# Sample attention of a hybrid decoder step: key pages in the prompt heads' memory, and key tiles that become the attention output's parts

## Chip, cores and metric

The kernel runs on one core of a Trainium2 chip, as one program. The metric is the device time of one execution in microseconds, given as the median of several runs. Beside each run stand the span of the profiled execution (from its first to its last recorded instruction) and the granted clock of the tensor engine.

## What is computed

One layer of a decoder trunk over 1024 prompt tokens and 64 sample tokens (8 sequences of 8). The mixer between two feed-forward networks has two branches, and each branch's output is gated:

```python
h = x + 0.5 * rms_norm(swiglu(rms_norm(x)))
q_sb, k_sb, v_sb, q_r, k_r, v_r, g_r, a_sb, a_r = split(rms_norm(h) @ w_in)
o_sb = stick_breaking(q_sb, keys, vals)        # 8 heads of 64
o_r  = silu(g_r) * head_norm(retention(rope(q_r), rope(k_r), v_r))
m = sigmoid(a_sb) * (o_sb @ w_sb_out) + sigmoid(a_r) * (o_r @ w_ret_out)
h = h + rms_norm(m @ w_o)
h = h + 0.5 * rms_norm(swiglu(rms_norm(h)))
```

For a sample, keys and values are 2048 cached positions, in 16 pages of 128 that a page table picks out of a pool, and its own new ones. Stick-breaking attention multiplies each sigmoid weight by a running product over the later positions, so logits are worked off from the newest page backwards.

## The kernel before

Precision first: nearly every large product is made of three matmuls (`mm3`, lines 133, 137, 138), on a high and a low part of each operand. The high part is made by ACT (line 96), the low part by DVE or POOL (line 99). This splitting is work that stands ahead of the matmuls all over the kernel.

The stages follow each other: the first FFN up to about 830 us; then the projections, retention and the prompt's attention (`prompt_sb`, to about 1642 us); the samples' attention (`decode_sb`, 1642 to 1940); `mixer_out` (1940 to 2097); the second FFN.

In `prompt_sb` each head holds its queries, two key parts and values in a pool `pqk` with three buffers, so three heads' tensors are there at a time. `decode_sb` opens its pools `decp` (pages: 6 buffers for keys, 5 for values, half a megabyte each), `deck` (the new keys kn, the query tile qd and two tiles kt of turned keys) and `dec` behind that. Pages come by indirect DMAs, which POOL issues (`gather`).

The samples go in four blocks of two sequences. `logits` of block g+1 runs beside `values` of block g (`both`). A key page is turned by transposes on the tensor engine (line 1202), copied from PSUM into kt by ACT or DVE in turn, and multiplied with qd (`product`, through line 1115). `stick` makes the weights bt out of a bank of logits; `weights` turns them again into at, which `values` multiplies with the value pages. A product is put off by one page group (`late`), a turn of weights by another (`todo`), and both lists are emptied at a block's end. qd is one tile: its 288 columns are cleared once by POOL (line 1106), and ACT fills in the eight query pieces of each block (line 1133).

The order on each engine is fixed when the program is built, and is for the most part that of the code. To cover waits, `through(gen, k)` puts k steps of other products, called fills, behind each step of a generator; the table `FILL_DEC` gives k for the five passes (the first logits, three mixed passes, the last values). A fill is one k-step, three matmuls, of the gates or of the product with w_ret_out (`gate_steps`, `ret_steps`), in the banks pa. For the latter the retention's output is loaded in three parts (`ul<-orT`, line 843) and split by ACT and DVE between the steps (`prep_step`).

At the end the samples' outputs odec are written into the last 64 columns of the DRAM tensor osT (line 1275), where the prompt's lie already. `mixer_out` loads osT in three column parts, sq (line 1528: 512, 288 and 288 columns), splits them into sh and sl, and multiplies them with w_sb_out into the two banks pa. DVE multiplies each result with a gate loaded from gaT (line 1545), adds the retention's from mrT (line 1546) and splits it into mh and ml, the input of the product with w_o, whose results ACT copies out as y (line 1561). y, normed, is split into the quarters q of the second FFN's input. SP issues all plain DMAs in program order, on eight lanes in turn; a DMA waits for the one eight places before it.

Of the kernel before, what the change touches and what calls it, by code (L numbers as in the profile page):

```python
# [19 lines left out]
P = 128  # L20
# [23 lines left out]
FILL_DEC = (.6, .8, .8, .8, .6)  # L44
# [24 lines left out]
class Trunk:  # L69
# [99 lines left out]
    def setup(self):  # L169
# [17 lines left out]
        self.osT = self.t(self.dram, [512, T], "osT")  # L187
# [700 lines left out]
    def prompt_sb(self):  # L888
        nc, io = self.nc, self.io
        win = io["w_in"][0]  # L890
        with ExitStack() as ctx:
            qp = self.pool("pqk", ctx)
# [12 lines left out]
            def proj(p):  # L905

                qs = [self.t(qp, [P, TP], "qs", F32R, bufs=3) for e in range(2)]
                kh = [self.t(qp, [P, TP], "kh", F32R, bufs=3) for e in range(2)]
                kl = [self.t(qp, [P, TP], "kl", F32R, bufs=3) for e in range(2)]
                vs = [self.t(qp, [P, 8, P], "vs", F32R, bufs=3) for e in range(2)]  # L910
# [159 lines left out]
    def decode_sb(self):  # L1070
# [5 lines left out]
        with ExitStack() as ctx:  # L1076
            pp = self.pool("decp", ctx)
            kp_ = self.pool("deck", ctx)
            dp = self.pool("dec", ctx)
# [11 lines left out]
            kn = self.t(kp_, [P, 4, TD], "kn")  # L1091
# [32 lines left out]

            def logits(g, ats):


                qv = qd.rearrange("q (b x) -> q b x", x=144)[:, :, :P].rearrange("q b (m y) -> q b m y", y=32)
# [31 lines left out]
                def new_keys():  # L1160
# [4 lines left out]
                    bt = self.t(dp, [P, TD], "btn")  # L1165
# [5 lines left out]
                    nc.scalar.activation(atn[:TD], tp[:TD, :P], AF.Copy)  # L1171
# [11 lines left out]
                def product(ps, b2, j, kt):  # L1183
                    side_by_side(ps, partial(query, b2), lambda m: kt[:, m, :], b2 == 0, b2 == 1)
                    if b2:
                        bt = self.t(dp, [P, 512], "bt", bufs=2)
                        left[0] = stick(bt, ps.rearrange("q (h i x) -> q h x i", h=2, i=2), 512, left[0])
                        todo.append((j, bt))

                late, todo, left = [], [], [None]  # L1190
                nk = new_keys()
                step = 0
                for j in range(NG - 1, -1, -1):
                    ps = self.bank("pb")
                    for b2 in range(2):
                        kp = [gather(self.t(pp, [P, 1024], "page", bufs=6), ck, 2 * g + b2, 2 * j + x)
                              for x in range(2)]
                        kt = self.t(kp_, [P, 4, 512], "kt", bufs=2)
                        for m in range(4):
# [18 lines left out]
                        late.append((ps, b2, j, kt))  # L1218
# [615 lines left out]
```

## Time and profile before

| | us |
|---|---|
| median of 3 runs | 2893.32 |
| lowest and highest run | 2891.1 and 2895.43 |
| the profiled execution | 2891.72 |
| its span | 2889.2 |
| PE busy in the span | 2798.6 (97%) |
| DVE, ACT, POOL busy | 2017.1, 1245.3, 738.5 |

The mean granted clock of the profiled execution is 0.99. In the profile PE is the tensor engine's matmuls, PEld its weight loads, DVE the vector engine, ACT the scalar engine, POOL GpSimd and SP the engine that issues most DMAs. An idle time is put down to what ended it, after the sign "<-". The time around the span is 2.5 us.

### The profile page before, as it was taken

To read this page: it belongs to the slowest core of one execution; us is meant where nothing else is said; L and a number is where in the kernel's file an instruction comes from. 1 tells how busy PE (TensorE), PEld (TensorE's weight loads), DVE (VectorE), ACT (ScalarE), POOL (GpSimd) and SP (SyncE) were. 2 spreads that over 40 slices of the span, in tenths; PEclk is the share of its full clock that TensorE was granted. 3 is DMA by queue.
4 is the path that set the end of the run, shared out by engine and by line. 5 is a ranking of instruction groups with operands and counts; after the bars stand their busy time and mean duration, and the time that the engine had idled before them with its cause. 6 is when DMAs were issued, how large, how long until landed. Compare 5 with 4: busy or idle time off the path is not lost.

```text
span 2889.2 us, 51617 instructions
## 1 busy us (share of the span) xinstructions
PE 2798.6 (97%) x20064; PEld 2633.3 (91%) x20064; DVE 2017.1 (70%) x3922; ACT 1245.3 (43%) x2546; POOL 738.5 (26%) x679
## 2 busy tenths in 40 slices
PE   7999999999999999999999889989999999999998
PEld 7898899999999999989999867768989988999997
DVE  7888878888753553546888744436578888688776
ACT  6444444444343333335666543213354444544443
POOL 0234513333150000000000245520013334233321
PEclk9999999999999999999999999999999999999999
DMA  6444444333252322333222389876333336333431
GB/s 177 145 127 144 140 155 123 110 112 108 80 162 83 99 84 86 94 113 80 76 74 76 123 294 332 297 244 198 105 96 121 119 110 189 122 103 107 130 89 42
DMA packets 420420, 380.63 MB, mean 132 GB/s; under 512 B 30352, under 2 KB 380944, under 8 KB 420176
## 3 DMA queue, kind: packets, MB, share of 16 engines
q1 hardware_dynamic: 397904, 306.03, 34.6%
q0 software_dynamic: 22272, 71.31, 7.4%
q8 instruction: 157, 2.57, 0.4%
q14 instruction: 87, 0.71, 0.1%
HBM read 310.03 MB, written 63.05 MB: 129 GB/s over the span
## 4 chain that ended last, share of the span: by engine, by line
PE 59%; DVE 5%; DMA 3%; issue 2%; POOL 1%; ACT 1%; SPq 0%; DVEq 0%; POOLq 0%; ACTq 0%
PE pa L133 10%; PE pa L138 10%; PE pa L137 10%; PE pb L133 3%; PE pb L138 3%; PE pb L137 3%; PE pc L137 3%; PE pc L138 3%; PE pc L133 3%; PE pc L1202 2%; PE pm L1011 1%; PE pm L1115 1%; PE pc L999 1%; DVE sl L99 1%; DMA ul<-orT 1%
## 5 line engine op out<-in xcount | busy, mean ns | idle before, releaser
L96 ACT ACTIVATE sh<-wr 128x512 fp32r<-128x512 f32 x592 | 340.0, 624 | 364.1 <-POOL wr L590 135.5
L133 PE MATMUL pa<-uh,wh 128*128 128x384 f32 (+1 forms) x1408 | 476.7, 339 | 4.2 <-ACT qdec L920 2.0
L138 PE MATMUL pa<-uh,wl 128*128 128x384 f32 (+1 forms) x1408 | 464.4, 330 | 0.0
L137 PE MATMUL pa<-ul,wh 128*128 128x384 f32 (+1 forms) x1408 | 463.5, 329 | 0.4 <-POOL ul L99 0.4
L99 DVE TENSOR_TENSOR sl<-wr,sh 128x512 fp32r<-128x512 f32 x592 | 398.8, 701 | 60.2 <-ACT sh L96 56.8
L133 PE MATMUL pa<-q,sh 128*128 128x256 f32 (+1 forms) x1408 | 410.4, 292 | 15.7 <-DVE p L648 7.8
L137 PE MATMUL pa<-q,sh 128*128 128x256 f32 (+1 forms) x1408 | 409.5, 291 | 2.2 <-DVE q L99 2.2
L138 PE MATMUL pa<-q,sl 128*128 128x256 f32 (+1 forms) x1408 | 408.5, 290 | 0.3 <-DVE sl L99 0.3
L137 PE MATMUL pc<-hl,whd 128*128 128x256 f32 (+2 forms) x1088 | 350.4, 324 | 2.6 <-DVE hl L99 2.6
L138 PE MATMUL pc<-hh,wld 128*128 128x256 f32 (+2 forms) x1088 | 350.0, 323 | 0.0
L133 PE MATMUL pc<-hh,whd 128*128 128x256 f32 (+2 forms) x1088 | 343.6, 324 | 4.5 <-DVE y L718 2.5
L718 DVE TENSOR_TENSOR y<-y,pc 128x256 f32<-128x256 f32 (+2 forms) x496 | 250.1, 516 | 135.8 <-PE pc L138 133.9
L133 PE MATMUL pb<-q,sh 128*128 128x288 f32 (+1 forms) x1088 | 314.8, 290 | 6.5 <-ACT sh L96 4.9
L138 PE MATMUL pb<-q,sl 128*128 128x288 f32 (+1 forms) x1088 | 314.6, 289 | 0.5 <-DVE sl L99 0.4
L137 PE MATMUL pb<-q,sh 128*128 128x288 f32 (+1 forms) x1088 | 314.9, 290 | 0.0
L133 PEld LDWEIGHTS pa<-q,sh 128*128 128x128 f32 x1408 | 268.2, 191 | 20.8 <-DVE p L648 8.8
L133 PEld LDWEIGHTS pa<-uh,wh 128*128 128x128 f32 x1408 | 265.7, 189 | 20.1 <-issue 10.0
L137 PEld LDWEIGHTS pa<-q,sh 128*128 128x128 f32 x1408 | 268.0, 190 | 4.7 <-DVE q L99 2.7
L137 PEld LDWEIGHTS pa<-ul,wh 128*128 128x128 f32 x1408 | 265.7, 189 | 3.3 <-issue 1.4
L138 PEld LDWEIGHTS pa<-q,sl 128*128 128x128 f32 x1408 | 267.2, 190 | 1.5 <-DVE sl L99 0.5
L138 PEld LDWEIGHTS pa<-uh,wl 128*128 128x128 f32 x1408 | 265.2, 188 | 2.7 <-issue 1.7
L588 POOL TENSOR_TENSOR wr<-wr 128x512 f32<-128x512 f32 x76 | 108.2, 1424 | 495.5 <-DVE sl L99 495.4
(340 smaller groups left out, 5958.3 us busy)
## 6 DMA issues: line engine op xcount, KB each, us to landing
wr<-in_w_ffn_gu_dram SPq DMA_DIRECT2D x176, 512.0 KB
wrd<-in_w_ffn_down_dram SPq DMA_DIRECT2D x88, 512.0 KB
wr<-in_w_in_dram SPq DMA_DIRECT2D x56, 512.0 KB
q<-cB SPq DMA_DIRECT2D x16, 576.0 KB
wr<-in_w_o_dram SPq DMA_DIRECT2D x10, 512.0 KB
cB<-y SPq DMA_DIRECT2D x32, 144.0 KB
cB<-xr SPq DMA_DIRECT2D x32, 144.0 KB
s<-in_state_ret_dram SPq DMA_DIRECT2D x16, 256.0 KB
```

The costliest lines, as they stand in the source:

```text
L96: return self.nc.scalar.activation(dst, src, AF.Copy)
L99: (eng or self.nc.vector).tensor_tensor(dst, src, hi.bitcast(F32), op=ALU.subtract)
L133: ins = mm(ps, wh, xh, start=first, stop=False)
L137: mm(ps, wh, xl, start=False, stop=False)
L138: mm(ps, wl, xh, start=False, stop=last)
L588: tt(v1, v0, v1, op=ALU.add)
L718: nc.vector.tensor_tensor(y[p][:, d, c], y[p][:, d, c], ps[:, :n], op=ALU.add)
L999: nc.tensor.transpose(tp[:, j * P : (j + 1) * P], bt[:, j * P : (j + 1) * P], self.ident)
L1011: ins = nc.tensor.matmul(po[:, lo:256], vs[:, j, :], ats[j // 4][x][:, j % 4, lo:256], start=(j == 0 and x == 0), stop=(j == last and x == 1))
L1115: return nc.tensor.matmul(out[32 * m : 32 * m + 32], w(m), x(m), start=first, stop=last, skip_group_check=True)
L1202: ins = nc.tensor.transpose(tp[:, i * P : (i + 1) * P], kp[i // 2][:, (i % 2) * 512 + m * P : (i % 2) * 512 + (m + 1) * P], self.ident)
```

## The change

Memory: the prompt's pool becomes three pools, pqk0 to pqk2, one for each head that is held. In the samples' stage their room holds three pools: dec2 has key pages 0 to 3; dec1 value pages 0 to 3; dec0 has kn, the two tiles qd, btn, one atn, key pages 4 and 5 and value page 4. A page can be fetched as soon as the heads that lay there have been read for the last time. The two tiles kt lie at the other end of memory, in a pool that stays open into `mixer_out`, where they become sh and sl of the first 512 columns.

Work: `late` and `todo` are no longer emptied at the end of a block; the next block's steps take them up, and a new generator `last_block`, which runs beside the last values, takes the last ones and then loads and splits the prompt's 512 columns of osT. The samples' outputs go to a DRAM tensor of their own, osD. atn and vnew have 64 rows in place of 128, which removes three memsets. In `mixer_out` the pools m1 and mg change places, and the parts 1 and 2 are loaded whole (two DMAs for each, and two for the samples' columns) and split ahead of the first product. `FILL_DEC` has other values.

```diff
-FILL_DEC = (.6, .8, .8, .8, .6)
+FILL_DEC = (.8, .8, .8, .75, .5)
...
-        self.osT = self.t(self.dram, [512, T], "osT")
+        self.osT = self.t(self.dram, [512, TP], "osT")
+        self.osD = self.t(self.dram, [512, TD], "osD")
...
-            qp = self.pool("pqk", ctx)
+            places = [self.pool(f"pqk{i}", ctx) for i in range(3)]
...
+                at = [places[(2 * p + e) % 3] for e in range(2)]
...
-            pp = self.pool("decp", ctx)
-            kp_ = self.pool("deck", ctx)
-            dp = self.pool("dec", ctx)
+            p0, p1, p2, dp = (self.pool(x, ctx) for x in ("dec0", "dec1", "dec2", "dec"))
+            key_pages = [(p2, f"kp{i}") for i in range(4)] + [(p0, f"kp{i}") for i in range(4, 6)]
+            value_pages = [(p1, f"vp{i}") for i in range(4)] + [(p0, "vp4")]
+            with self.tc.using_default_side("right"):
+                self.kpc = ExitStack()
+                kp_ = self.pool("deck", self.kpc)
+            key_parts = [(kp_, f"kt{i}") for i in range(2)]
...
-            qd = self.t(kp_, [P, 288], "qd")
-            nc.gpsimd.memset(qd, 0.0)
-            atns = [self.t(dp, [P, P], f"atn{x}") for x in range(2)]
+            qds = [self.t(p0, [P, 288], f"qd{x}") for x in range(2)]
             for x in range(2):
-                nc.gpsimd.memset(atns[x][64:128], 0.0)
+                nc.gpsimd.memset(qds[x], 0.0)
+            atns = [self.t((p0, dp)[x], [TD, P], f"atn{x}") for x in range(2)]
...
                             if late and m == 1:
-                                product(*late.pop(0))
+                                late.pop(0)()
                             if todo and b2 == 1:
-                                weights(*todo.pop(0))
+                                todo.pop(0)()
...
-                while late:
-                    product(*late.pop(0))
+            def last_block():
+                late.pop(0)()
+                for _ in range(4):
+                    yield
+                todo.pop(0)()
                 yield
-                while todo:
-                    weights(*todo.pop(0))
+                sh, sl = (in_turn(key_parts, [P, 4, 512], F32R) for _ in range(2))
+                self.first = sh, sl
+                self.attn_parts(sh, sl, 0, 512)
                 yield
...
-                    self.through(values(g, ats), FILL_DEC[4])
+                    self.through(both(last_block(), values(g, ats)), FILL_DEC[4])
...
-            nc.sync.dma_start(self.osT.rearrange("(m q) t -> q m t", q=P)[:, :, TP:T], ost)
+            nc.sync.dma_start(self.osD.rearrange("(m q) t -> q m t", q=P), ost)
...
+    def attn_parts(self, sh, sl, o, n):
+        lf = sl.bitcast(F32)
+        m = min(n, TP - o)
+        for q in range(0, 4, 2):
+            qq = slice(q * P, (q + 2) * P)
+            self.nc.sync.dma_start(lf[:, q : q + 2, :m], self.osT[qq, o : o + m].rearrange("(k p) t -> p k t", p=P))
+            if m < n:
+                self.nc.sync.dma_start(lf[:, q : q + 2, m:], self.osD[qq, :].rearrange("(k p) t -> p k t", p=P))
+        for q in range(4):
+            self.hi(sh[:, q, :], lf[:, q, :])
+            self.lo(sl[:, q, :], lf[:, q, :], sh[:, q, :])
...
             m0 = self.pool("m0", ctx)
+            m1 = self.pool("m1", ctx)
             gp = self.pool("mg", ctx)
-            m1 = self.pool("m1", ctx)
```

What this does to the order on three engines. POOL at the start of the samples, before (page and vpage are gathered pages, wl a weight's low part for a fill):

```order
L99 TENSOR_TENSOR wl_3508_19147<-wr_3506_19144,wh_3507_19146 128x1024
L1109 MEMSET atn0_3517_19205 64x128
...
L1100 DMA page_3520_19214<-in_cache_k_dram,rowix_4_75 128x1024
...
L1100 DMA page_3541_19314<-in_cache_k_dram,rowix_4_75 128x1024
L1100 DMA vpage_3619_19719<-in_cache_v_dram,rowix_4_75 128x1024
...
L1100 DMA vpage_3646_19901<-in_cache_v_dram,rowix_4_75 128x1024
L99 TENSOR_TENSOR wl_3669_20020<-wr_3667_20017,wh_3668_20019 128x1024
L1106 MEMSET qd_3516_19203 128x288
```

POOL there with the change (kp and vp are the pages):

```order
L1113 DMA kp0_3522_19228<-in_cache_k_dram,rowix_4_75 128x1024
...
L1113 DMA kp3_3533_19285<-in_cache_k_dram,rowix_4_75 128x1024
L99 TENSOR_TENSOR wl_3509_19155<-wr_3507_19152,wh_3508_19154 128x1024
L1120 MEMSET qd0_3517_19217 128x288
...
L1113 DMA kp4_3543_19333<-in_cache_k_dram,rowix_4_75 128x1024
L1113 DMA kp5_3544_19335<-in_cache_k_dram,rowix_4_75 128x1024
L1113 DMA vp4_3649_19931<-in_cache_v_dram,rowix_4_75 128x1024
L1113 DMA vp0_3623_19751<-in_cache_v_dram,rowix_4_75 128x1024
...
L1113 DMA vp3_3646_19900<-in_cache_v_dram,rowix_4_75 128x1024
L99 TENSOR_TENSOR wl_3662_19990<-wr_3660_19987,wh_3661_19989 128x1024
```

The first gathers stand ahead of the first weight split, and the memsets of qd between the gathers in place of behind them all.

SP at the end of the samples, before (wr is raw w_o, mrT and gaT are the gates' rows):

```order
L146 DMA wr_4119_22958<-in_w_o_dram 128x8x128
L1275 DMA osT_8_79<-odec_3513_19195 128x4x64
L1528 DMA sq_4013_22306<-osT_8_79 128x512
L874 DMA mrT_13_84<-gs_4000_22268 128x320
...
L1528 DMA sq_4016_22318<-osT_8_79 128x512
L1542 DMA xr_4038_22391<-gaT_10_81 128x512
L1544 DMA xr_4039_22393<-mrT_13_84 128x512
```

SP there with the change:

```order
L1296 DMA osD_9_80<-odec_3514_19209 128x4x64
L146 DMA wr_4110_22959<-in_w_o_dram 128x8x128
L1536 DMA sl1_4013_22329<-osT_8_79 128x2x288
...
L1536 DMA sl2_4015_22341<-osT_8_79 128x2x224
L1538 DMA sl2_4015_22341<-osD_9_80 128x2x64
...
L1538 DMA sl2_4015_22341<-osD_9_80 128x2x64
L146 DMA wr_4114_22991<-in_w_o_dram 128x8x128
L1572 DMA xr_4029_22391<-gaT_11_82 128x512
```

The loads of gates, xr, now stand behind the loads of both later parts and behind one more load of w_o.

ACT at the start of the second FFN, before (q are the FFN's input quarters, sh weight parts, pb the last products with w_o):

```order
L1561 ACTIVATE y1_4110_22890<-pb_4184_23488 128x288
...
L96 ACTIVATE q00_4195_23719<-y0_4109_22886 128x256
...
L1561 ACTIVATE y1_4110_22890<-pb_4189_23546 128x288
L96 ACTIVATE q01_4197_23721<-y0_4109_22886 128x256
...
L1561 ACTIVATE y1_4110_22890<-pb_4190_23572 128x288
L96 ACTIVATE sh_4211_23766<-wr_4209_23762 128x512
...
L1561 ACTIVATE y1_4110_22890<-pb_4191_23598 128x288
```

ACT there with the change:

```order
L1592 ACTIVATE y1_4101_22891<-pb_4181_23573 128x288
L96 ACTIVATE sh_4202_23767<-wr_4200_23763 128x512
...
L1592 ACTIVATE y1_4101_22891<-pb_4184_23651 128x288
L1592 ACTIVATE y1_4101_22891<-pb_4185_23677 128x288
L96 ACTIVATE q00_4186_23720<-y0_4100_22887 128x256 x4
...
L96 ACTIVATE q02_4190_23724<-y0_4100_22887 128x256 x4
L96 ACTIVATE sh_4215_23856<-wr_4213_23852 128x512
```

The sixteen splits of y stand behind the last copy out of pb, in place of between the tenth and the twelfth of its sixteen.

## Rows read from the trace of the kernel before

**Rows 1.** The page: the span, and busy time by engine (share of the span, instructions).
```profile
span 2889.2 us, 51617 instructions
...
PE 2798.6 (97%) x20064; PEld 2633.3 (91%) x20064; DVE 2017.1 (70%) x3922; ACT 1245.3 (43%) x2546; POOL 738.5 (26%) x679
```

**Rows 2.** Waits of PE, 1600 to 2120 us: total us, times, longest.
```profile
PE pc L999 <- DVE pt L1047: 3.3, 2, 2.0
PE pc L1115 <- POOL qd L1106: 3.1, 1, 3.1
PE pc L1179 <- DVE bt L1157: 3.0, 1, 3.0
...
PE pc L1202 <- DVE at L1180: 2.0, 1, 2.0
PE pc L1202 <- ACT btn L1152: 1.4, 1, 1.4
```

**Rows 3.** Three windows: length, busy us by engine, PEclk, DMA share, GB/s.
```profile
1640.00:1660.00 20.00, 16.65 (x103) 15.67 (x104) 2.49 (x6) 4.71 (x12) 13.42 (x15) 0.84 0.81 298
1716.00:1915.00 199.00, 198.79 (x1984) 149.38 (x1986) 89.20 (x152) 58.30 (x107) 105.19 (x96) 1.00 0.87 300
1940.00:1960.00 20.00, 12.04 (x45) 9.19 (x44) 11.40 (x20) 7.15 (x14) 0.00 (x0) 0.83 0.87 289
```

**Rows 4.** Timeline of POOL: start, us, engine, operation [idle before <- releaser].
```profile
1640.28 0.34 POOL L1109 MEMSET atn<- 64x128 f32 x2 [23.47 <-DVE bt L1050]
...
1654.95 2.34 POOL L99 TENSOR_TENSOR wl<-wr,wh 128x1024 fp32r<-128x1024 f32 x1
1657.24 0.34 POOL L1106 MEMSET qd<- 128x288 f32 x1
```

**Rows 5.** Timeline of PE around the wait on qd: page transposes.
```profile
1653.69 1.03 PE L1202 MATMUL pc<-ident,page 128*128 128x128 f32 x8
...
1658.67 1.97 PE L1202 MATMUL pc<-ident,page 128*128 128x128 f32 x8
```

**Rows 6.** Chain of waits through the first block: start, us, what.
```profile
1669.09 6.69 DMA ul<-orT
...
1703.15 11.22 DMA ul<-orT
```

**Rows 7.** Timeline of ACT: the copies into qd.
```profile
1657.61 0.70 ACT L1133 ACTIVATE qd<-qdec 64x32 f32<-64x32 f32 x4 [2.47 <-POOL qd L1106]
```

**Rows 8.** Timeline of PE at the start of mixer_out.
```profile
1947.88 1.22 PE L133 MATMUL pa<-sh,wh 128*128 128x512 f32 x2 [7.64 <-ACT sh L96]
1948.90 0.63 PE L137 MATMUL pa<-sl,wh 128*128 128x512 f32 x1
...
1955.66 0.51 PE L133 MATMUL pa<-sh,wh 128*128 128x512 f32 x1 [0.32 <-DVE xr L1545]
1956.00 0.40 PE L137 MATMUL pa<-sl,wh 128*128 128x512 f32 x1
```

**Rows 9.** Chain of waits at the end of the samples: start, us, what.
```profile
1935.07 4.11 DMA wr<-in_w_o_dram
...
1942.99 4.12 DMA sq<-osT
```

**Rows 10.** Timeline of DVE and SP there (SPq issues DMAs).
```profile
1940.38 1.22 DVE L99 TENSOR_TENSOR wlo<-wr,who 128x1024 fp32r<-128x1024 f32 x1 [3.17 <-ACT who L96]
...
1942.12 0.52 SPq L1275 DMA_DIRECT2D osT<-odec  x1
...
1945.41 0.43 SPq L1542 DMA_DIRECT2D xr<-gaT  x1
```

**Rows 11.** Timeline of ACT and DVE at the second FFN's start.
```profile
2077.51 2.65 ACT L96 ACTIVATE q<-y 128x256 fp32r<-128x256 f32 x8
...
2081.94 5.45 DVE L99 TENSOR_TENSOR q<-y,q 128x256 fp32r<-128x256 f32 x16
...
2096.80 0.41 ACT L1561 ACTIVATE y<-pb 128x288 f32<-128x288 f32 x1 [2.79 <-PE pb L138]
```

More of the change, by code (lines that the diff above doesn't have):

```diff
@@ L905, in proj @@
             def proj(p):
[L907 to L910, printed above, removed]
+                at = [places[(2 * p + e) % 3] for e in range(2)]
+                qs = [self.t(x, [P, TP], "qs", F32R) for x in at]
+                kh = [self.t(x, [P, TP], "kh", F32R) for x in at]
+                kl = [self.t(x, [P, TP], "kl", F32R) for x in at]
+                vs = [self.t(x, [P, 8, P], "vs", F32R) for x in at]
                 for e in range(2):
@@ L1076, in decode_sb, with in_turn @@
         with ExitStack() as ctx:
-            pp = self.pool("decp", ctx)
-            kp_ = self.pool("deck", ctx)
-            dp = self.pool("dec", ctx)
+            p0, p1, p2, dp = (self.pool(x, ctx) for x in ("dec0", "dec1", "dec2", "dec"))
[5 more added lines that the diff above has]
+            key_parts = [(kp_, f"kt{i}") for i in range(2)]
+            def in_turn(places, shape, dtype=F32):
+                places.append(places.pop(0))
+                return self.t(places[-1][0], shape, places[-1][1], dtype)
             mask = self.t(dp, [P, 4, TD], "dmask")
@@ L1089, in decode_sb @@
             ost = self.t(dp, [P, 4, TD], "odec")
-            kn = self.t(kp_, [P, 4, TD], "kn")
+            kn = self.t(p0, [P, 4, TD], "kn")
             tp = self.bank("pc")
@@ L1123, in side_by_side @@
                 return ins
+            late, todo = [], []
             def logits(g, ats):
+                qd = qds[g % 2]
                 qv = qd.rearrange("q (b x) -> q b x", x=144)[:, :, :P].rearrange("q b (m y) -> q b m y", y=32)
@@ L1170, in new_keys @@
                     nc.tensor.transpose(tp[:TD, :P], bt, self.ident)
-                    nc.scalar.activation(atn[:TD], tp[:TD, :P], AF.Copy)
+                    nc.scalar.activation(atn, tp[:TD, :P], AF.Copy)
                     ats[NG] = atn
@@ L1187, in product @@
                         left[0] = stick(bt, ps.rearrange("q (h i x) -> q h x i", h=2, i=2), 512, left[0])
-                        todo.append((j, bt))
-                late, todo, left = [], [], [None]
+                        todo.append(partial(weights, j, bt))
+                left = [None]
                 nk = new_keys()
@@ L1195, in logits @@
                     for b2 in range(2):
-                        kp = [gather(self.t(pp, [P, 1024], "page", bufs=6), ck, 2 * g + b2, 2 * j + x)
+                        kp = [gather(in_turn(key_pages, [P, 1024]), ck, 2 * g + b2, 2 * j + x)
                               for x in range(2)]
-                        kt = self.t(kp_, [P, 4, 512], "kt", bufs=2)
+                        kt = in_turn(key_parts, [P, 4, 512])
                         for m in range(4):
@@ L1217, in logits @@
                             yield
-                        late.append((ps, b2, j, kt))
-                while late:
-                    product(*late.pop(0))
+                        late.append(partial(product, ps, b2, j, kt))
+            def last_block():
[3 more added lines that the diff above has]
+                todo.pop(0)()
                 yield
-                while todo:
-                    weights(*todo.pop(0))
+                sh, sl = (in_turn(key_parts, [P, 4, 512], F32R) for _ in range(2))
+                self.first = sh, sl
+                self.attn_parts(sh, sl, 0, 512)
                 yield
@@ L1500, in mixer_in @@
                 self.knew = self.t(kp, [64, 512], "knew")
-                self.vnew = self.t(kp, [P, 512], "vnew")
+                self.vnew = self.t(kp, [64, 512], "vnew")
                 self.qdec = self.t(kp, [P, 4, TD], "qdec")
-                nc.gpsimd.memset(self.vnew[64:128, :], 0.0)
                 self.prompt_sb()
@@ L1514, in mixer_out @@
             m0 = self.pool("m0", ctx)
+            m1 = self.pool("m1", ctx)
             gp = self.pool("mg", ctx)
[L1516 removed]
+            self.t(gp, [P, 512], "sq", bufs=4)
             wp = self.pool("mw", ctx, bufs=2)
@@ L1522, in mixer_out @@
                 sh, sl = {}, {}
-                for c, (o, n) in reversed(list(enumerate(mch))):
+                sh[0], sl[0] = self.first
+                for c, (o, n) in list(enumerate(mch))[1:]:
                     sh[c], sl[c] = (self.t(op, [P, 4, n], f"s{x}{c}", F32R) for x in "hl")
-                for c, (o, n) in enumerate(mch):
-                    for q in range(4):
-                        raw = self.t(gp, [P, 512], "sq", bufs=4)
-                        nc.sync.dma_start(raw[:, :n], self.osT[q * P : (q + 1) * P, o : o + n])
-                        self.hi(sh[c][:, q, :n], raw[:, :n])
-                        self.lo(sl[c][:, q, :n], raw[:, :n], sh[c][:, q, :n])
+                    self.attn_parts(sh[c], sl[c], o, n)
                 w1 = [self.unit(io["w_sb_out"][0][:, j * 256 : (j + 1) * 256].rearrange("(k p) c -> p k c", p=P))
@@ L1548, in mixer_out @@
                         self.lo(ml[c][:, d, :n], m[:, :n], mh[c][:, d, :n])
+            self.kpc.close()
             y, pl, yc = self.right()
```

4 lines of the change are left out of this document (2 added, 2 removed).

## The prediction

> **What bounds the kernel now.** I read the page first: the tensor engine is busy for 97% of a span of 2889.2 us [rows 1], so a change that leaves the matmuls as they are can only win back idle time of that engine, or time in which its clock was low. The list of its waits from 1600 to 2120 us then says how much lies in the stages that the diff touches [rows 2]: besides the row of 3.3 us on the prompt's last splits there are 3.1, 3.0, 2.0 and 1.4 us around the first sample block, and one long wait at the end of the samples' stage, 7.64 us ahead of the first product with w_sb_out [rows 8]. Third, the table of windows [rows 3]: between 1716 and 1915 us the engine is busy for 198.79 of 199 us, so in the middle of the stage there is nothing to win, though the DMA engines are there at a share of 0.87; around the first and the last wait the granted clock is 0.84 and 0.83, that is, part of those windows ran at the lower of the two levels. The waits are priced with what follows them: after the wait on qd, eight page transposes take 1.97 us where the same eight took 1.03 us before it [rows 5]; after the 7.64 us, a 512-wide matmul takes 0.63 us where it later takes 0.40 [rows 8], for eight matmuls, about 1.8 us.
>
> The forecast is a sum against the profiled execution, 2891.7 us (2889.2 of span and 2.5 around it). The median of the runs shown, 2893.3, lies 1.6 us above it.
>
> **Start of the samples: +3.3 us.** Before, POOL runs two memsets of atn at 1640.28, held for 23.47 us by the prompt's last split, then eleven gathers, then a weight split of 2.34 us at 1654.95, and only then the memset of qd at 1657.24 [rows 4]; the tensor engine waits 3.1 us for it. Now the memsets of qd stand ahead of seven of the gathers, behind a wait that the prompt releases early. The 3.1 us go, and with them 0.9 us of low clock (1.97 less 1.03). Against it: the eight small ACT copies into qd, 0.70 us for four [rows 7], now run beside the prompt's last splits, for which the tensor engine is already waiting; I charge 0.7. Bounds 2.6 (all 1.4 us charged) to 4.0.
>
> **First block: +2.0 us.** The 2.0 us wait at 1678 is behind ACT and DVE, which split the first retention part when its load lands, 6.69 us after issue at 1669.09 [rows 6]. Now most gathers are issued before the prompt ends, so they no longer share the DMA engines with the loads behind them, and the fills that free this load's buffer are spent sooner (.8 of a fill a step in place of .6); I estimate an issue near 1660, 9 us earlier. The stall loses its cause, but the same splits could hold an earlier product: between -2.0 and +3.5 (2.0 and as much low clock as in the first case, rounded up).
>
> **First block edge: +2.0 us.** The logits' tail is no longer drained at the block's end; the last product and the last weights become the first work of the next block, with fills between them. That aims at the 3.0 us (transposes right behind the scan that makes bt) and touches the 1.4 us. The second retention part still arrives there, 11.22 us after issue in the trace [rows 6], and holds ACT in its queue. Of 4.4 us I take a little under half; bounds 0 and 4.4.
>
> **Last block: -0.3 us.** The splits of the prompt's part (four of ACT, four of DVE, same sizes as before) now stand inside the last block, two of DVE's ahead of the copy that makes the last weights. The transposes and the copy have fills around them, and two of the four DVE splits come only behind the copy; nothing to 3.0 us, which is what such transposes waited at the first block's edge [rows 2], taken near the small end.
>
> **End of the samples: +2.5 us.** This is the largest term. Call the end of the last fill t0: 1947.88 less 7.64, or 1940.24. Before, the third row of outputs (d = 2) starts at 1955.66, t0 + 15.4 [rows 8]. Now the first two rows need only the prompt's part and start at t0. The third needs one of two PSUM banks back, and for that DVE must multiply by a gate (line 1575 in the new text). Two chains stand ahead of that multiply. *On DVE*: eight splits of parts 1 and 2, the last four of which wait for osD to be written and read back. The odec copies no longer stand behind the w_o split that ran at 1940.38 [rows 10], so the write is issued at about t0 - 1.3; taking 4.1 us for each landing (the w_o and sq rows of the chain [rows 9]), 0.7 us of issuing and 2.2 us of splits, the multiply is free at t0 - 1.3 + 4.1 + 0.7 + 4.1 + 2.2 = t0 + 9.8. *On SP*: the loads of gates stand behind the fourth w_o load, which waits for the third to land; the third is issued when the split of 1940.38 is over, t0 + 1.4, so the gate is issued at t0 + 5.9 and lands at t0 + 10.0 (before, the first gate's load was issued at 1945.41, t0 + 5.2, and hidden [rows 10]). With 0.7 us for the multiply the third row starts at t0 + 10.7; the first two rows take 24 matmuls, 5.6 us at the full clock (7.78 from 1947.88 to 1955.66, less 0.3 of waiting and 1.8 of low clock). That is a new wait of some 5.1 us, and it brings the 1.8 us of low clock with it again, which the 15.4 already contained: 15.4 - 10.7 - 1.8 = 2.9, taken as 2.5, since the loads share the engines. Bounds: with landings of 6.69 us, the slower row, the DVE chain gives t0 + 15.7 and a loss of 2.1; with landings of half the rows' 4.1 a gain of about 7.
>
> For pieces this small the rows show only a floor: the write of odec has the same 256-byte pieces and nothing waited for it. The Trainium skill (DMA: Bandwidth & Descriptors, Specifications) says that transfers under 512 B are done as read-modify-write and do not reach line rate, which speaks against the new 256-byte reads from osD: by it this term would lie towards its lower bound. The same page (Anatomy of one DMA) puts the fixed part of a transfer at about 2.0 us; by that alone the multiply would start near t0 + 7.6, the term would be 5.3, and the sum 11.0. The 4.1 us of the rows, under load, decide.
>
> **Start of the second FFN: -1.3 us.** Pools m1 and mg change places, so the quarters of the FFN's input now lie over m1, which is read up to the last product with w_o. Before, ACT's splits of y ran from 2077.51, long before the last eviction at 2096.80 [rows 11], and matmuls of the FFN stood between those of w_o. Now all sixteen follow the last eviction: 0.41 for it, 0.33 for the first high part (2.65 by 8), 0.34 for the first low part (5.45 by 16), or 1.1 us, and 0.2 for the next weights' splits behind them. Bounds 0.5 and 3.0.
>
> **Sum.** 3.3 + 2.0 + 2.0 - 0.3 + 2.5 - 1.3 = 8.2 us: 2883.5 on the profiled scale, **2885.1** as a median. The terms' bounds give about 2875 at the good end, of which I take 2877; all bad ends together, -7.5, would be 2901; two thirds of the way there, some 2896, is as far as I think several of them go at once.
>
> **Rivals.** *(1) The waits only move.* ACT's retention splits hold other products, the edge keeps its 4.4 us, and the third row of outputs waits as long as the first did: only the start and the FFN count, 3.3 - 1.3 = 2.0, which gives 2891.3, no change. For it: the load latencies are the same DMAs in the same queues. Against: two of the waits have causes that are simply gone. Chance 0.28.
> *(2) The stalls vanish.* Gates arrive early and the parts are split in time: 3.1 + 3.0 + 2.0 + 1.4 + 7.6 + 0.9 + 1.8 = 19.8 us, 2873.5. Against: the two chains above. Chance 0.08.
> *(3) Pages come late in the last two blocks.* The fill rates go from .8 to .75 over 69 steps and from .6 over 35 steps to .5 over 41, while the first block takes more: some 5 us of cover leave the last two blocks, where the DMA engines already have a share of 0.87 [rows 3]. If that share reaches 1.0 there, the tensor engine waits for pages, 5 us and about 0.9 us of low clock after each of four waits, 3.6; and the same load makes each landing 6.69 us, so the end term falls by 4.6 to -2.1. Then 8.2 - 13.2 = -5.0, or with the last block's 3.0 us in place of 0.3, -7.7: 2901, slower. It decides where these blocks show waits on pages and less than full busy time; before, at 0.87, they show 0.21 us of idle time in 199. Chance 0.12.
> My forecast has 0.52.
>
> **How the numbers follow.** A change under about 0.2% (5.8 us) cannot be told from none in a measurement of this kernel: faster is below 2887.5, slower above 2899.1. The forecast's own spread puts about a seventh of it above 2887.5 (0.07): faster 0.45 + 0.08 = 0.53, same 0.07 + 0.28 = 0.35, slower 0.12. The range from 2877 to 2896.5 leaves out the second and third rivals.
>
> **What would show it.** No wait on qd near the first sample block and the DMA share spread over the prompt's last 20 us; the first w_sb_out product without a wait, then one of 4 to 7 us ahead of the third row on DVE (sl or xr); a wait of about 1 us on ACT or DVE's q at the first matmul of the second FFN. I am wrong if the third row does not wait, if the middle blocks show waits on pages, or if the FFN's start costs more than 3 us.

## The result, and the profile after

The change is a little slower: 2899.48 us (median of 9 runs, 2893.3 to 2903.56) against 2893.32 (9 runs), a ratio of 1.0022 with a 95% interval from 1.0012 to 1.0032. The forecast was 2885.1, with a range from 2877 to 2896.5, so the result lies above it.

The page of the change, first the span, then busy time by engine:

```profile
span 2895.6 us, 51608 instructions
...
PE 2810.4 (97%) x20064; PEld 2631.2 (91%) x20064; DVE 2016.8 (70%) x3922; ACT 1242.2 (43%) x2546; POOL 737.2 (25%) x677
```

The span is 6.4 us longer [rows 1], but the tensor engine is not idle for longer: its busy time grew by 11.8 us at the same 20064 matmuls, so it idles for 5.4 us less. The loss lies in busy time. To find its place, both executions are cut at the same four instructions: the transposes of the new keys (the start of the samples' stage), the end of the last fill (t0), the first matmul of the third row of outputs, and the fourth hidden tile of the second FFN (its multiply on DVE).

| | before, us | change, us | difference |
|---|---|---|---|
| start to the samples' stage | 1641.24 | 1641.62 | +0.4 |
| samples' stage, to t0 | 299.00 | 303.94 | +4.9 |
| t0 to the third row of outputs | 15.42 | 13.36 | -2.1 |
| third row to the fourth hidden tile | 164.19 | 167.50 | +3.3 |

The windows of the samples' stage (length, busy us of PE, PEld, DVE, ACT, POOL, then PEclk, DMA share, GB/s), before:

```profile
1641.24:1940.24 299.00, 286.72 (x2761) 219.71 (x2760) 124.32 (x216) 90.18 (x170) 146.32 (x136) 0.98 0.85 294
```

and with the change:

```profile
1641.62:1945.56 303.94, 296.39 (x2761) 216.15 (x2761) 126.84 (x222) 90.34 (x166) 133.88 (x125) 1.00 0.81 276
```

The same number of matmuls, 2761, keeps the engine busy for 9.67 us more, although the granted clock is higher (1.00 against 0.98) and the idle time fell from 12.28 to 7.55 us. So the waits did go, as the list of PE's waits between 1600 and 2150 us says; beside it stand [rows 2]:

```profile
PE pa L133 <- DVE xr L1575: 7.6, 1, 7.6
PE pc L1217 <- ACT kt L1224: 3.8, 3, 1.8
PE pc L1001 <- DVE pt L1049: 3.2, 2, 2.0
PE pb L1127 <- DVE kt L1222: 2.6, 1, 2.6
...
PE pa L133 <- ACT q L96: 0.8, 1, 0.8
...
PE pc L1217 <- ACT btn L1167: 0.3, 1, 0.3
PE pc L1217 <- DVE at L1195: 0.3, 1, 0.3
```

No wait on qd is left, none on bt at the first block's edge, and the wait on at is 0.3 in place of 2.0. In their place are 3.8 and 2.6 us on the copies of turned keys into kt. The first row is the new one ahead of the third row of outputs.

Where the busy time went is read from the timeline of PE. A stretch of the change (start, us):

```profile
1773.83 0.31 PE L137 MATMUL pa<-ul,wh 128*128 128x320 f32 x1
1773.97 0.31 PE L138 MATMUL pa<-uh,wl 128*128 128x320 f32 x1
1774.21 0.43 PE L1127 MATMUL pm<-vp,at 128*32 128x128 f32 x8
1774.57 0.41 PE L133 MATMUL pa<-uh,wh 128*128 128x320 f32 x1
1774.82 0.30 PE L137 MATMUL pa<-ul,wh 128*128 128x320 f32 x1
1774.96 0.31 PE L138 MATMUL pa<-uh,wl 128*128 128x320 f32 x1
```

A k-step's three matmuls of 128x320 follow each other at 0.15 us. Here the third one, at 1773.97, is followed after 0.24 us by eight narrow matmuls of a value product (128*32: 32 output columns of the array, four side by side), the next fill starts 0.36 us after them, and its first matmul takes 0.25. The kernel before has fewer such single lots. Counted over the samples' stage in the order of PE, it has 105 separate runs of narrow matmuls, 65 of them a single lot of eight; the change has 129, and 93 of them single. A long run of the kernel before:

```profile
1772.23 1.74 PE L1115 MATMUL pm<-vpage,at 128*32 128x128 f32 x56
1773.90 0.74 PE L1179 MATMUL pc<-ident,bt 128*128 128x128 f32 x4
```

56 narrow matmuls in 1.67 us are 0.030 each, 0.24 for eight. A separate lot of eight among fills thus costs 0.09 us ahead of it, 0.12 behind it, and 0.10 on the next full matmul: 0.31 us for each change to narrow matmuls and back. Every single lot of eight value matmuls between two fills takes 0.36 us from its start to the next fill's, 26 times before and 46 times with the change.

The same reckoning over the whole stage takes, for each run, the spacings from the last full matmul ahead of it to the second one behind it, without idle time, and subtracts the median spacings that the same matmuls have among their like in all thirteen traces. It gives 31.2 us for the 105 runs before and 38.3 us for the 129 of the change, 0.30 us a run in both, so 7.1 of the 9.67 us lie there. Some 3.7 us more lie in one place of the change, where the order has pulled a product with kt apart and set matmuls of the new keys' value product (vnew) between its pairs:

```profile
1727.10 1.04 PE L1127 MATMUL pb<-kt,qd 128*32 128x512 f32 x2
1728.07 0.41 PE L1127 MATMUL pm<-vnew,atn 64*32 64x128 f32 x4
1728.41 1.04 PE L1127 MATMUL pb<-kt,qd 128*32 128x512 f32 x2
...
1731.03 1.05 PE L1127 MATMUL pb<-kt,qd 128*32 128x512 f32 x2
1732.00 0.74 PE L1194 MATMUL pc<-ident,bt 128*128 128x128 f32 x4
```

Each pair takes 0.97 us by itself, where all eight take 0.86 when they stand together. The whole place takes 4.9 us, the same matmuls in two lots about 1.2. The kernel before has no such place; experiments 3 and 4 below have the same one, 1 and 6 a smaller one, the others none. All other spacings of the stage together came to some 1.2 us less.

The Trainium skill (TensorEngine Tiling (Array Packing), Key Properties) has a rule that fits these rows: "Changing tiling mode (not just tile) drains the TensorE". It gives no price. By that rule the order of narrow and full matmuls counts, and the three gaps above are its price here as far as these spacings show it. Whether the drain itself makes the gaps, or the loading of the next weights, no run separates. The rule was there to be weighed before the prediction, and was not.

### The profile page after: what moved, and what is told of

It reads as the page before. It is cut to its first block, busy times and chain, and to the rows that moved or that the text cites. A ratio compares the mean times of both kernels' runs of the same rounds, so it can differ in the third digit from the quotient of the medians.

```text
span 2895.6 us, 51608 instructions
## 1 busy us (share of the span) xinstructions
PE 2810.4 (97%) x20064; PEld 2631.2 (91%) x20064; DVE 2016.8 (70%) x3922; ACT 1242.2 (43%) x2546; POOL 737.2 (25%) x677
## 4 chain that ended last, share of the span: by engine, by line
PE 59%; DVE 5%; DMA 2%; issue 2%; POOL 1%; ACT 0%; SPq 0%; POOLq 0%; DVEq 0%; ACTq 0%
PE pa L133 10%; PE pa L138 10%; PE pa L137 10%; PE pb L133 3%; PE pb L138 3%; PE pb L137 3%; PE pc L137 3%; PE pc L138 3%; PE pc L133 3%; PE pc L1217 2%; PE pm L1013 1%; PE pc L1001 1%; PE pm L1127 1%; PE pb L1127 1%; DVE sl L99 1%
```

## The experiments

Two theories stood against each other. *Switching*: every separate run of narrow matmuls among full ones costs about 0.3 us, and the change cut the same work into more runs. *Place*: narrow matmuls became slower in themselves, because of where the pages now lie or what the DMA engines do beside them. Since the time up to the samples' stage varied from 1641 to 1648 us between executions of kernels that are all but the same up to there, the experiments are compared by stage, from one profiled execution of each. All ratios are to the kernel before on the same chip, with their 95% intervals. Experiments 1 to 4, 5 to 8 and 9 to 11 ran on three chips, where the kernel before has medians of 2894.71, 2901.37 and 2893.89 us; stages and ratios from different chips are compared with that reserve.

| kernel | runs | stage | PE busy | ratio |
|---|---|---|---|---|
| before | 105 | 299.00 | 286.72 | |
| change | 129 | 303.94 | 296.39 | 1.0022 (1.0012 to 1.0032) |
| 1 lists emptied | 96 | 298.49 | 286.42 | 1.0001 (0.9990 to 1.0013) |
| 2 before, lists carried | 120 | 306.14 | 294.43 | 1.0013 (1.0001 to 1.0024) |
| 3 gates first | 129 | 305.32 | 297.57 | 1.0016 (1.0004 to 1.0029) |
| 4 pools back | 129 | 302.70 | 297.04 | 0.9997 (0.9985 to 1.0008) |
| 5 before, fours | 78 | 321.02 | 289.31 | 1.0070 (1.0056 to 1.0084) |
| 6 emptied, pools back | 96 | 301.83 | 284.93 | 0.9970 (0.9959 to 0.9982) |
| 7 pairs, pools back | 92 | 295.21 | 284.37 | 0.9939 (0.9922 to 0.9956) |
| 8 fours, emptied, pools back | 75 | 320.41 | 288.10 | 1.0019 (1.0007 to 1.0031) |
| 9 before, carried, pairs | 92 | 287.19 | 280.72 | 0.9961 (0.9949 to 0.9973) |
| 10 before, pairs | 92 | 306.20 | 287.00 | 1.0027 (1.0017 to 1.0038) |
| 11 as 7, other rates | 87 | 298.11 | 284.48 | 0.9970 (0.9959 to 0.9982) |

**1. Lists emptied at the block's end again.**

```diff
                         late.append(partial(product, ps, b2, j, kt))
+                while late:
+                    late.pop(0)()
+                yield
+                while todo:
+                    todo.pop(0)()
+                yield
...
             def last_block():
-                late.pop(0)()
                 for _ in range(4):
                     yield
-                todo.pop(0)()
                 yield
```

> The change, but late and todo are emptied at each block's end again; memory, fill table and everything else stay. Theory (switching): a run of narrow matmuls (128*32) between full ones costs some 0.3 us, and the instruction order of the samples' stage has 96 such runs here, 129 in the change, 105 in the kernel before. So PE's busy time from the prompt's last transposes to the first w_sb_out product falls by about 33 x 0.31 = 10 us against the change's 295.8, some idle time comes back at the block's first edge (about 3), and the total falls by 5 to 9 us, to 2891 to 2895. Rival (place): narrow matmuls are slower because of where pages lie or of the gathers beside them; then busy time stays within 2 us of the change's and the total rises by the idle time that comes back, to 2900 to 2903.

Busy time fell by 10.0 us for 33 runs, idle time came back (12.1 us), and the total is that of the kernel before. The pages stayed where the change puts them, so *place* does not explain the busy time. The narrow matmuls themselves say the same: eight value matmuls inside a run take 0.242 us (median) before and with the change.

**2. The kernel before with the carried lists alone.**

```diff
                             if late and m == 1:
-                                product(*late.pop(0))
+                                late.pop(0)()
...
-            qd = self.t(kp_, [P, 288], "qd")
+            qds = [self.t(kp_, [P, 288], f"qd{x}") for x in range(2)]
...
-                while late:
-                    product(*late.pop(0))
-                yield
-                while todo:
-                    weights(*todo.pop(0))
-                yield
...
-                    self.through(values(g, ats), FILL_DEC[4])
+                    self.through(both(last_block(), values(g, ats)), FILL_DEC[4])
```

> The kernel before with only the carried lists: the last products and weights of a block are taken up by the next block's steps (two tiles qd, which that needs); memory, pages, fill table, osT and mixer_out as before. Order: 120 runs of narrow matmuls in place of 105. Theory (switching): PE busy in the samples' stage rises by about 15 x 0.31 = 4.7 us, the idle time there falls by 0 to 4 us, the total is 2893 to 2898. Rival (place): busy time unchanged within 1.5 us and the total falls by the idle time, to 2889 to 2893.

With the old memory, 15 runs more took 7.7 us more of busy time, and the total rose by 0.13%, barely clear of noise. The product with kt is not pulled apart here; the fill table is that of the kernel before. The two experiments undo and do the same part, from either kernel; the stage window of each, first experiment 1, then 2:

```profile
1641.31:1939.80 298.49, 286.42 (x2760) 221.27 (x2760) 124.88 (x220) 89.17 (x165) 135.81 (x125) 0.97 0.82 280
```

```profile
1646.10:1952.24 306.14, 294.43 (x2761) 219.97 (x2760) 121.76 (x218) 88.93 (x169) 144.27 (x137) 0.97 0.84 287
```

**3. Gates loaded first.** The loads and splits of parts 1 and 2 are pinned behind the second row of outputs (`beside` holds them behind what stands before them on each engine):

```diff
-                    self.attn_parts(sh[c], sl[c], o, n)
...
                         self.lo(ml[c][:, d, :n], m[:, :n], mh[c][:, d, :n])
+                        if c == 0 and d == 1:
+                            for x in (1, 2):
+                                self.beside(partial(self.attn_parts, sh[x], sl[x], *mch[x]),
+                                            PINNED + (mybir.EngineType.SP,))
```

> The change, but the loads and splits of parts 1 and 2 of the attention's output stand behind the first two rows of outputs of mixer_out on SP, ACT and DVE, so that the first gates are loaded ahead of them. If the 7.6 us wait of the third row is the gate's load behind these six loads (issued 6.6 us after the first product and 5.9 in flight), that wait falls to 2 to 4 us and the total by 3.5 to 5.5 us, to 2894 to 2896. If it is the fourth w_o load that holds the gate, the wait stays above 5.5 us and the total falls by less than 2.

A miss by halves: the wait fell from 7.59 to 4.95 us, the stretch from t0 to the fourth hidden tile from 180.86 to 178.45, and the total by too little to be told. Most of what held the gate was still there: it was issued 3.7 us behind t0, after two loads of w_o, and landed 6.16 us after issue, with none of the six loads ahead of it:

```profile
1951.67 0.37 SPq L146
1952.04 0.05 issue
1952.09 6.16 DMA xr<-gaT
```

**4. Pools m1 and mg in their old order.**

```diff
             m0 = self.pool("m0", ctx)
-            m1 = self.pool("m1", ctx)
             gp = self.pool("mg", ctx)
+            m1 = self.pool("m1", ctx)
```

> The change with the pools m1 and mg in their old order, so that the second FFN's input quarters lie over mg and m0 again and can be split before the last products with w_o. If the swap costs what the prediction says, the 0.8 us wait at the second FFN's first matmul goes and the time from the third row of outputs to that FFN's first hidden tiles falls by 1.3 to 2 us; the total by as much (2897.5 to 2898.2, hardly to be told in the total, so the profile decides). If the swap costs nothing, both stay as they are.

The wait on q went, but the stretch behind t0 fell by 3.9 us, twice what was expected, because the 7.6 us wait went too. SP's timeline shows how:

```profile
1949.46 0.43 SPq L1296 DMA_DIRECT2D osD<-odec  x1
1950.24 0.39 SPq L1572 DMA_DIRECT2D xr<-gaT  x1
1950.94 0.37 SPq L1536 DMA_DIRECT2D sl<-osT  x1
```

The first gate is issued 0.5 us ahead of t0 (1950.70), not 6.6 behind it. In the change the buffers of the gates, in mg, lie over the room of dec0 (kn, the tiles qd, key pages 4 and 5, value page 4); in the old order they do not. The trace of the change shows no wait for these tenants: the last value matmuls end at 1935.7, and the gate's load is issued at 1952.20. So the swap changes where SP has the gate's load in its order; that the shared places are the reason is not shown. Two smaller waits took its place, from the list of PE's waits:

```profile
PE pb L133 <- ACT mh L96: 2.7, 1, 2.7
PE pa L133 <- DVE gs L874: 2.3, 1, 2.3
```

**5. The kernel before with value products in fours.**

```diff
                             self.marks.append(ins.ins)
-                            yield
+                            if j == NG or i == 3:
+                                yield
```

> The kernel before with one edit of the order: four value products (two pages) are issued behind each other before the generator gives way to a fill, with fill rates raised to match (.6, 1.3, 1.3, 1.3, 1.9). No memory place, tensor or stage of mixer_out changes. Order: 78 runs of narrow matmuls in place of 105. Theory (switching, 0.31 us a run): PE busy in the samples' stage falls by about 8 us from 287.0, idle time may grow by 0 to 5 us since pages are needed in bigger lots; total 4 to 8 us below the kernel before. Rival (place and traffic decide the narrow matmuls' cost): busy time within 2 us of before, total the same or slower by the idle time.

Slower, against the expectation: the runs fell to 78, but idle time rose to 31.7 us, the granted clock over the stage fell to 0.95 (0.98 before), and busy time rose by 2.6 us. The largest waits are those at the block ends:

```profile
PE pc L1179 <- DVE bt L1157: 20.5, 4, 6.3
```

That no fills are left there for the last scan of a block, with fewer steps, is my reading and was not tested alone. This says nothing against switching, but neither for it.

**6. Lists emptied, pools back** (edits 1 and 4 together).

> The change with both parts that cost something undone: lists emptied at each block's end (96 runs of narrow matmuls) and m1 and mg in their old order. If the two costs are separate, the stretch from the prompt's last transposes to the second FFN's fourth hidden tile is that of the first experiment less what the fourth gained behind the samples' stage: 298.5 + 176.9 = 475.4 us against 478.6 before and 484.8 in the change; total 2 to 4 us below the kernel before. If they overlap, 478 to 480 and no difference in the total.

The costs did not overlap: the stretch took 472.10 us where 475.4 were expected, and the total fell by 0.30%, some 9 us, where 2 to 4 were expected. The sum hides two misses. The stage had 4.8 us more idle time than in the first experiment, and the stretch behind t0 took 170.27 us, far less than the 176.9 of the fourth; no wait is left ahead of the third row, and why is not shown.

**7. Value products in pairs, pools back, lists carried as in the change.**

```diff
-FILL_DEC = (.8, .8, .8, .75, .5)
+FILL_DEC = (.8, 1.08, 1.08, 1.02, .9)
...
                             self.marks.append(ins.ins)
-                            yield
+                            if j == NG or i % 2:
+                                yield
```

> The change with the lists carried over as it has them, m1 and mg in their old order, and value products issued in pairs (fill rates .8, 1.08, 1.08, 1.02, .9): 92 runs of narrow matmuls, so the carried lists without their cost. Theory (switching): the samples' stage takes 303.9 - 37 x 0.31 = 292.4 us with the change's idle time of about 7 us, the stretch to the fourth hidden tile 469, total 8 to 11 us below the kernel before. Rival: carrying itself (waits of ACT and DVE moved into other products) is what slows it, not the runs; then the stage stays above 299 us and the total is within 3 us of before.

Against the fourth experiment the pairs and their fill rates are the only difference in the kernel: 37 runs fewer and no product pulled apart, 12.7 us less of busy time (0.34 us a run), 5.2 us more idle, and 7.5 us off the stage. The stage took 2.8 us more than forecast, the stretch, 465.17 us, 3.8 less. Its ratio, 0.9939, is the lowest, and it beats both kernels; the total fell by some 17.5 us where 8 to 11 were forecast, though the stretch is only 13.4 us below that of the kernel before. Experiment 9, on another chip, has the lower median (2881.40 against 2883.82 us) and an interval that overlaps, so neither is shown to be the faster. The stage window of experiment 7:

```profile
1648.33:1943.54 295.21, 284.37 (x2760) 219.82 (x2760) 126.06 (x220) 89.41 (x166) 132.50 (x125) 1.00 0.83 285
```

**8. Lists emptied, fours, pools back.** Edits 1, 4 and 5, with the rates (.8, 1.28, 1.28, 1.28, 1.5).

> As the sixth experiment, with value products in fours (fill rates .8, 1.28, 1.28, 1.28, 1.5): 75 runs of narrow matmuls, lists emptied. Theory (switching): the stage takes 298.5 - 21 x 0.31 = 292 us, of it 12 us idle if the pages keep up; total 8 to 10 us below the kernel before. If pages in fours come too late, idle time rises by 3 to 6 us and the total is 3 to 6 below.

Refuted like the fifth, with the same waits: 17.7 us on bt, 3.9 on pages, and a clock of 0.94.

**9. The kernel before, lists carried, pairs** (edits 2 and 7 without the pools).

> The second experiment's kernel (memory, osT and mixer_out of the kernel before, lists carried over) with value products in pairs and the fill rates of the seventh: 92 runs of narrow matmuls in place of 120. Theory (switching, 0.31 to 0.42 us a run): the samples' stage falls from 306 to 295 to 298 us, the stretch to the fourth hidden tile from 484.3 to 473 to 476, total 3 to 6 us below the kernel before. What is then left to the seventh kernel (469 forecast, 465 measured) is the worth of the pages' places and of the early parts, 8 to 10 us. If the places are worth nothing, it comes within 2 us of the seventh.

The best stage of all, 287.19 us, and a total some 11 us below the kernel before, where 3 to 6 were expected:

```profile
1644.19:1931.38 287.19, 280.72 (x2761) 219.19 (x2760) 124.05 (x217) 89.21 (x171) 144.98 (x137) 0.99 0.87 306
```

Against the second experiment 28 runs fewer took 13.7 us of busy time away, 0.49 a run, more than expected, and 5 us of idle time. From the first transposes to the fourth hidden tile it took 467.58 us, the seventh 465.17: the new places and the early parts come to 2.4 us where I expected 8 to 10, from one execution of each on two chips, and by the medians experiment 9 is the one that is 2.4 us lower. No worth of theirs is shown. The stage itself is 8 us longer in the seventh; what it gains is the end, where this kernel still waits 7.5 us for the attention's first part.

**10. The kernel before with pairs alone** (rates .6, 1.08, 1.08, 1.08, 1.1).

> The kernel before with value products in pairs alone (fill rates .6, 1.08, 1.08, 1.08, 1.1), lists emptied at block ends: 92 runs in place of 105. Switching alone gives 4 to 5.5 us of busy time back; but with fewer steps the fills no longer stand behind the last scan of a block, where the experiment with fours waited 20.5 us in four waits. I expect 4 to 10 us more idle time on such waits (transposes of bt on DVE), and a total between 1 us below and 6 us above the kernel before. If pairing pays by itself, the total falls by more than 3.

In kind as expected: 11.6 us of waits on bt at block ends, 6.9 us more idle time in the stage, and a total 0.27% higher, at or a little above the upper end of the range (6.1 us by the medians, 7.8 by the ratio). But busy time did not fall for 13 runs fewer (287.00 us against 286.72, at a clock of 0.97 against 0.98). By the spacings the runs cost 3.7 us less, and the other matmuls took as much more. So in these runs carrying the lists paid only with fewer runs, and pairs only with the lists carried.

**11. As 7, with the rates (.6, 1.08, 1.08, 1.08, 1.0).**

> The seventh kernel with other fill rates (.6, 1.08, 1.08, 1.08, 1.0): 87 runs of narrow matmuls in place of 92. Theory (switching): busy time in the samples' stage 1.5 to 2 us less than the seventh's 284.2, idle time the same or up to 3 more because the first block has fewer fills; total within 3 us of the seventh's.

Five runs fewer brought nothing: busy time the same where 1.5 to 2 us less were expected, 2.8 us more idle, a clock of 0.97 against 1.00, each on its own chip.

## Why the prediction was wrong

**The step that failed** is the first: "a change that leaves the matmuls as they are can only win back idle time of that engine, or time in which its clock was low". The change leaves the matmuls (those with vnew have 64 rows in place of 128), but not their neighbours. Carrying late and todo over spreads the narrow products singly among fills, as experiments 1 and 2 show from either side; the new fill rates were not tested alone. The sum has no term for that, and it is the largest one: 9.7 us more of busy time, at a slightly higher clock. Of it 7.1 us are the 24 runs more and some 3.7 us the product that was pulled apart, less some 1.2 us elsewhere. What it rests on could have been read before: the trace of before has lots of 56 at 0.030 us and single lots at 0.36 for eight, and the two orders have 105 and 129 runs. I compared the orders for what waits on what, and not for what stands beside what.

**Start, first block, edge, last block**: 7.0 us were forecast, in idle time and low clock. Idle time in the stage fell by 4.7, and the clock of the two windows around the first block rose:

```profile
1640.00:1660.00 20.00, 19.40 (x134) 18.55 (x135) 3.56 (x7) 5.04 (x9) 5.22 (x4) 0.89 0.28 74
1660.00:1680.00 20.00, 17.11 (x149) 12.08 (x149) 11.97 (x25) 9.53 (x20) 6.51 (x7) 1.00 0.83 278
```

Before, the window from 1640 us had 0.84 [rows 3] and that from 1660 us 0.93. The waits that were to go did go; part of the gain was given back to the copies into kt, which the forecast had as a possible wait, by a range and not by name.

**End of the samples**: +2.5 was forecast, a new wait of 5.1 us ahead of the third row, at t0 + 10.7. It was 7.59 us, at t0 + 13.4, again with a few matmuls at the low clock behind it (0.63 us each). From PE's timeline:

```profile
1945.56 0.40 PE L133 MATMUL pa<-kt,wh 128*128 128x512 f32 x1
...
1958.92 0.79 PE L133 MATMUL pa<-kt,wh 128*128 128x512 f32 x1 [7.59 <-DVE xr L1575]
1959.51 0.63 PE L137 MATMUL pa<-kt,wh 128*128 128x512 f32 x1
```

The chain of waits shows why:

```profile
1947.79 4.40 DMA sl<-osT
1952.20 5.88 DMA xr<-gaT
1958.18 0.70 DVE xr L1575
```

The gate was issued 6.6 us after t0 (5.9 was forecast) behind the loads that were named. What released it was the landing of the first load of sl, which stands eight places before it on SP. The gate landed 5.88 us after the start of its issue, not the 4.1 taken from the rows. Part of that is the issue itself, which took SP 1.77 us; the other issues there take about 0.4. The loads ahead of it are not shown to be the cause, since the gate of experiment 3 had none of them ahead and took 6.16 us. The place was right, the size wrong, and the cause was only half seen: experiment 4 shows that the order of m1 and mg decides when a gate is loaded. The third row came 2.1 us earlier than before, and 1.2 us of low clock follow it, so the term comes to about +0.9.

The Trainium skill (DMA: Bandwidth & Descriptors, Anatomy of one DMA) has a fixed part of about 2.0 us, in a section on transfers that GpSimd issues, while the gate's load is issued by SP. It was further off still than the 4.1. Taken alone it would start the multiply near t0 + 5.8 (an estimate); the prediction's 7.6 has a part for the size in it. For the read-modify-write rule that the prediction names no run gives a separate price: the loads from osD landed with those beside them.

**Start of the second FFN**: -1.3 was forecast; the wait came as said, ACT's splits behind the last copy:

```profile
2101.25 0.41 ACT L1592 ACTIVATE y<-pb 128x288 f32<-128x288 f32 x1 [2.76 <-PE pb L138]
2101.56 5.01 ACT L96 ACTIVATE q<-y 128x256 fp32r<-128x256 f32 x16
2106.48 2.70 ACT L96 ACTIVATE sh<-wr 128x512 fp32r<-128x512 f32 x5
```

The first matmul starts at 2102.02 after a wait of 0.8 us. The whole stretch behind the third row lost 3.3 us, of which 1.2 are low clock (six matmuls at 0.43 us for 0.23): -2.1, inside the bounds. But the swap of the pools was priced for this place alone. Undone, it gave back 3.9 us behind t0 in experiment 4, and the end of the samples was the larger share, which the price of the swap left out.

**The rivals**: none of the three is what happened, though one mark of the first came: the third row waited as long as the first had (7.59 us, 7.64 before). The slower one was to be pages that come late; the DMA share of the stage fell instead (0.81 against 0.85), and PE's waits on pages came to 0.2 us. That its 2901 lies near the measured time is chance. No sign of being wrong that the prediction named explains the miss either. The forecast's own terms as measured (4.7 of idle time in the stage, +0.9 and -2.1) still add up to a gain of 3.5 us; less the 9.7 us of busy time they give -6.2, against the -6.4 of the span.

## What to carry to other kernels

When a change reorders an engine that is busy all the time, count in both instruction orders how often it changes between the kinds that cost a change, here full and narrow matmuls, and whether matmuls that run side by side still stand together, and price a change from the trace by spacing, not by durations: a neighbour can cost more than a wait. A wait that is removed may have been what bunched cheap work together; put the bunching into the code, as the pairs do, before taking the wait away. And two pools that change places can move loads in the order of the engine that issues them (experiment 4): compare that order for every tenant, not only for the one that is to gain.

## What the runs showed of the hardware that was not expected

- Busy time of the tensor engine is not fixed by its matmuls: 2761 in the same stage took between 280.72 and 297.57 us at a granted clock of 0.99 (experiments 9 and 3), in different orders.
- A change from full matmuls to narrow ones side by side and back costs about 0.31 us at the full clock, by the spacings shown. Over whole stages the spacings give 0.29 to 0.31 us a run in ten of the thirteen traces, and 0.33 to 0.36 in experiments 5, 7 and 8. Busy time between kernels that differ in one edit came to 0.30 (experiment 1), 0.34 (7 against 4), 0.49 (9 against 2) and 0.51 us a run (2); the upper values hold more than the changes themselves, such as the clock of 0.97 in 2 and the product pulled apart in 4.
- Narrow matmuls that run side by side lose by being pulled apart: a pair with kt took 0.97 us by itself in the change, all eight together 0.86.
- Waiting went with a low clock: in experiments 5 and 8 the idle time of the samples' stage (about 32 us in each) came with a granted clock of 0.95 and 0.94 over the stage, and busy time did not fall although the runs did.
